# Fourteen priorities of a greedy scheduler that writes the order of every engine, in a hybrid decoder layer

## The chip, the cores and the metric

The kernel runs on one core of a Trainium2 chip. The metric is the device time of one execution in microseconds (us): the median of three runs of the kernel before is 645.49 us (645.2 to 647.72). The engines are TensorE (PE: matmuls and transposes), VectorE (DVE), ScalarE (ACT), GpSimd (POOL) and SyncE (SP, which only issues transfers). Each engine works through its own instructions strictly in the order in which the program lists them.

## The reference, cut to what matters

One layer on 512 tokens of width 1024, in float32:

- a norm and one input projection to 1816 columns: 512 for a state-space mixer (S5), 512 for the queries, 768 for keys and values of three attention branches, 24 for gates;
- the S5 mixer: a complex diagonal recurrence per 16-channel group, then GELU and a gated linear unit (GLU) with a 512 x 512 matrix;
- the attention: a compressed branch (31 block summaries), a selected branch and a window branch. At this length the selected and the window branch both come to full causal attention, each with its own keys and values. Each head's three results are mixed with sigmoid gates;
- two norms, the output projection, the residual;
- a mixture of experts: 4 groups, the best group per token, the best 2 of its 8 experts, each a gated MLP of inner width 256. The weights of all 32 experts are 100 MB and must all be read.

## The kernel before, in words

**How work is written.** Each part of the layer is a Python generator (`proj`, `scores`, `gelu`, ...). It yields one instruction at a time, or a `Seq` of matmuls, sometimes with several engines to choose from (`Any`, and `cp`, line 399 on, which offers ACT, DVE and sometimes POOL). It can also yield a condition (a buffer must be free, a flag must be set). All generators run interleaved in one planner, `Sched` (line 112). All instructions carry line 234 in the profile, the planner's `issue`.

**What sets the order.** The planner has a cost and a latency for every kind of instruction. For the next instruction of every generator that isn't held by a condition, `pick` finds the earliest time `s` at which its engine is free and its inputs are there. Then `run` takes the one with the least sum of start and priority, and writes it at the end of its engine's list (lines 299 and 300):

```
if best is None or s + h[1] < best[0]:
    best = (s + h[1], s, f, h)
```

`h[1]` is the generator's entry in `PRIO`. A lower number means: taken first. A priority of -0.6 against -0.1 wins where the other could start up to 0.5 us earlier, all in the planner's own time. A generator that waits for a flag is not in the comparison until the planner has written the instruction after which the flag is set.

**The stages.** (1) `wload`, `xsplit`, `wsplit` and `proj` make the projection in three-term float32r products; beside it run `s5` (tables of the recurrence), the sinks (`sink_u`, `sink_k`, `sink_q`, `sink_gt` for the gates) and `compress`. (2) S5 in four rounds r = 0 to 3: `s5a` (tables per round, four transposes each through PSUM kind `g`, evacuated as `EP<-g`), `s5in`, `s5b` (matmuls `g<-FT,w`, recurrence `w<-r,w` on DVE), `gelu` (steps `w<-w` of 128 x 512; after rounds 1 and 3 it transposes through `g` and copies out as `sa<-g`, 128 x 256), then `glu`, whose end opens ten more 1 MB slots (`sb`) beside the thirteen of `sa`. (3) Attention: `scores` (matmuls into `a`, row maximum, exponential into a tile P of 1 MB), `scale` (P times gate over row sum: `mx` steps on four columns, then four multiplies `sa<-sa,mx` of 128 x up to 512 per unit), `values` (transposes `t<-ident,sa`, evacuation `pts<-t`, matmuls `o<-pts,sa`), `cmp` (the compressed branch, tiles `ct`), `finish`. A unit is a query block (3 to 0), a branch and a head group; only four P tiles exist (`NP`), and `values` must read a unit before its P is free again. PSUM has three buffers of kind `a`, two of `t`, one of `o`, two of `g`, shared by all. (4) `wo` and `outproj` with `resid`; `norm2`, `top2` and `place` per block of 128 tokens, `route`, `weights`. (5) The experts: `static` for 16 tiles of 128 tokens (two experts each), `spill` for one overflow tile. Six tiles (`SC`) are added into the residual on PE by `scatter`; the others by an indirect transfer that adds into the output in memory.

**The weights of the experts.** `prefetch` (line 469) issues 96 transfers of 1 MB on SP's queue, each as soon as a slot is free beyond those that `need` keeps for other parts. `static` frees a slot when its matmuls have read it.

Of the kernel before, what the change touches and what calls it, by code (L numbers as in the profile page):

```python
# [27 lines left out]
for _n, _w in (("g1", 8), ("lre", 48), ("lim", 48), ("lst", 48), ("dsk", 8), ("bglu", 4), ("gq", 1),  # L28
# [16 lines left out]

PRIO = {"proj": -3.72, "wsplit": 0.29, "xsplit": -0.08, "norm1": 0.04, "sink_u": 0.55, "sink_q": -0.76,
        "sink_gt": 3.61, "sink_k": -0.06, "s5": 0.19, "s5a": -0.69, "bcload": -9.42, "toeplitz": -18.02,
        "s5in": -0.17, "gelu": -0.12, "s5b": -0.75, "glu": -1.41, "compress": -0.96, "scores": -0.93,  # L50
        "scale": 0.37, "values": -0.25, "cmp": 0, "finish": -0.24, "wo": -1.28, "outproj": 0.02, "resid": -0.73,
        "norm2": -29.18, "top2": -0.61, "weights": 1.96, "place": -109.89, "prep": 1.2, "route": -1.71,
        "consts": -11.11, "scatter": -0.86, "base": -5.49, "moe": 43.94, "master": -5.48, "start": -35.5,
        "wload": -4.37, "prefetch": 3.58, "static": 2.45, "spill": -2.7}

# [54 lines left out]
class Sched:  # L112
# [12 lines left out]
    def spawn(self, gen, bias=0.0):  # L125
        self.th.append([gen, PRIO.get(gen.__name__, 0.0) + bias, None, None])

# [1981 lines left out]
```

## Time and profile before

| what | value |
|---|---|
| median of three runs | 645.49 us |
| the profiled execution | 649.24 us, of it 647.4 us span |
| PE busy | 542.4 us (84%) |
| DVE busy | 369.0 us (57%) |
| ACT busy | 229.9 us (36%) |
| POOL busy | 126.5 us (20%) |
| read from memory / written | 138.9 MB / 13.6 MB |

The profiled execution lies 3.75 us above the median of the runs. The page cuts the span into 40 slices and gives each engine's busy share in tenths; a table of busy time by stage is made by giving the profile the stage limits. In a timeline row stand start, duration, engine, operation, output and inputs by the program's names with the shape, the number of instructions merged, and in brackets the engine's idle time before the row with what ended it.

### The profile page before, as it was taken

To read this page: it belongs to the slowest core of one execution; us is meant where nothing else is said; L and a number is where in the kernel's file an instruction comes from. 1 tells how busy PE (TensorE), PEld (TensorE's weight loads), DVE (VectorE), ACT (ScalarE), POOL (GpSimd) and SP (SyncE) were. 2 spreads that over 40 slices of the span, in tenths; PEclk is the share of its full clock that TensorE was granted. 3 is DMA by queue.
4 is the path that set the end of the run, shared out by engine and by line. 5 is a ranking of instruction groups with operands and counts; after the bars stand their busy time and mean duration, and the time that the engine had idled before them with its cause. 6 is when DMAs were issued, how large, how long until landed. Compare 5 with 4: busy or idle time off the path is not lost. (4 is left out here: it accounts for less than half of the span.)

```text
span 647.4 us, 8863 instructions
## 1 busy us (share of the span) xinstructions
PE 542.4 (84%) x3071; PEld 328.1 (51%) x3071; DVE 369.0 (57%) x1076; ACT 229.9 (36%) x513; POOL 126.5 (20%) x143
## 2 busy tenths in 40 slices
PE   3979968973968996999997369799999999999673
PEld 2869937862545665676686233344343443434120
DVE  6898989889897987978656951002141340414000
ACT  6425123453735764767233021124212122221001
POOL 1020110442620305003232021202101010211010
PEclk9979979995977997999999569989999999999887
DMA  6543444420201101614987958999999999999993
GB/s 202 156 134 102 112 123 114 135 62 8 42 5 36 42 26 58 266 66 139 411 344 265 376 195 313 382 391 386 420 388 397 409 387 420 387 420 352 326 316 53
DMA packets 39742, 148.40 MB, mean 229 GB/s; under 512 B 9488, under 2 KB 16528, under 8 KB 27024
## 3 DMA queue, kind: packets, MB, share of 16 engines
q1 hardware_dynamic: 32928, 129.46, 52.8%
q0 software_dynamic: 5040, 15.21, 9.5%
q10 hardware_dynamic: 1728, 3.15, 1.3%
q8 instruction: 25, 0.41, 0.3%
q14 instruction: 21, 0.17, 0.1%
HBM read 138.92 MB, written 13.60 MB: 236 GB/s over the span
## 5 line engine op out<-in xcount | busy, mean ns | idle before, releaser
L234 PE MATMUL a<-sa 128*128 128x256 f32 (+4 forms) x608 | 113.7, 330 | 18.9 <-ACT sa L234 14.5
L234 PEld LDWEIGHTS a<-sa 128*128 128x128 f32 (+1 forms) x608 | 86.8, 196 | 34.7 <-ACT sa L234 17.9
L234 PE MATMUL a<-sa,sb 128*64 128x512 f32 (+1 forms) x324 | 96.2, 594 | 1.3 <-DMA sa<-in_we 1.3
L234 DVE TENSOR_TENSOR h<-a,h 128x256 f32<-128x256 f32 x17 | 7.2, 425 | 132.2 <-ACT h L234 132.2
L234 PE MATMUL a<-sb 128*64 128x512 f32 (+1 forms) x204 | 73.5, 624 | 3.0 <-DMA sb<-in_we 3.0
L234 PE MATMUL a<-sa,hT 128*64 128x512 f32 (+1 forms) x168 | 57.0, 599 | 1.7 <-ACT hT L234 0.9
L234 PEld LDWEIGHTS a<-sa,sb 128*64 128x64 f32 (+1 forms) x324 | 29.5, 141 | 48.1 <-issue 45.4
L234 ACT ACTIVATE h<-a 128x256 f32<-128x256 f32 x17 | 6.5, 384 | 111.0 <-PE a L234 111.0
L234 POOL DMA_INDIRECT out<-sc,oi x10 | 16.0, 1600 | 124.9 <-ACT sc L234 80.2
L234 PEld LDWEIGHTS a<-sb 128*64 128x64 f32 (+1 forms) x204 | 22.0, 150 | 30.1 <-issue 24.8
L234 ACT ACTIVATE sb<-t 128x512 f32<-128x512 f32 x42 | 23.6, 595 | 23.2 <-PE t L234 22.8
L234 POOL DMA_INDIRECT sc<-h2d,gi x16 | 16.5, 1033 | 78.0 <-PE t L234 59.3
L234 PE MATMUL a<-sb,hT 128*64 128x512 f32 x80 | 30.1, 600 | 0.5 <-ACT hT L234 0.5
L234 ACT ACTIVATE sa<-a,mx 128x512 f32<-128x512 f32 (+3 forms) x48 | 27.1, 573 | 8.5 <-DVE mx L234 7.9
L234 PE MATMUL o<-sa 128*128 128x256 f32 x192 | 28.4, 284 | 1.1 <-DVE xr L234 1.1
L234 DVE SCALAR_TENSOR_TENSOR sa<-a,tabw,sa 128x512 fp32r<-128x512 f32 x12 | 9.0, 751 | 35.5 <-ACT sa L234 25.5
L234 DVE TENSOR_REDUCE mx<-a 128x1 f32<-128x512 f32 (+3 forms) x44 | 27.0, 635 | 3.0 <-PE a L234 3.0
L234 PE MATMUL g<-sb,sa 128*128 128x512 f32 x104 | 27.7, 404 | 0.0
L234 ACT ACTIVATE pts<-t 128x512 f32<-128x512 f32 (+1 forms) x35 | 20.4, 595 | 18.1 <-PE t L234 18.1
L234 PE MATMUL t<-ident,sc 128*128 128x128 f32 x136 | 21.7, 306 | 5.3 <-DMA sc<-h2d,g1i 4.1
L234 PEld LDWEIGHTS o<-sa 128*128 128x128 f32 x192 | 25.3, 191 | 1.6 <-DVE xr L234 1.5
L234 PEld LDWEIGHTS t<-ident,sc 128*128 128x128 f32 x136 | 16.6, 155 | 18.4 <-issue 13.0
(391 smaller groups left out, 1046.3 us busy)
## 6 DMA issues: line engine op xcount, KB each, us to landing
sa<-in_we SPq DMA_DIRECT2D x58, 1024.0 KB, 22.6
sb<-in_we SPq DMA_DIRECT2D x33, 1024.0 KB, 16.4
raw<-in_win SPq DMA_DIRECT2D x14, 512.0 KB, 3.8
sc<-in_we SPq DMA_DIRECT2D x5, 1024.0 KB
sb<-in_wout SPq DMA_DIRECT2D x6, 512.0 KB, 7.4
xr<-in_xt SPq DMA_DIRECT2D x4, 512.0 KB, 5.3
sa<-in_wck SPq DMA_DIRECT2D x8, 256.0 KB, 3.0
sa<-in_wcv SPq DMA_DIRECT2D x8, 256.0 KB, 3.6
```

The costliest lines, as they stand in the source:

```text
L234: inst = getattr(e.real, fn)(*a, **k)
```

## The change

Fourteen entries of `PRIO` get other numbers. Nothing else differs: the same instructions, tiles, buffers and transfers, in another order on each queue, and, where several engines were offered, perhaps on another engine.

```diff
-PRIO = {"proj": -3.72, "wsplit": 0.29, "xsplit": -0.08, "norm1": 0.04, "sink_u": 0.55, "sink_q": -0.76,
-        "sink_gt": 3.61, "sink_k": -0.06, "s5": 0.19, "s5a": -0.69, "bcload": -9.42, "toeplitz": -18.02,
-        "s5in": -0.17, "gelu": -0.12, "s5b": -0.75, "glu": -1.41, "compress": -0.96, "scores": -0.93,
-        "scale": 0.37, "values": -0.25, "cmp": 0, "finish": -0.24, "wo": -1.28, "outproj": 0.02, "resid": -0.73,
-        "norm2": -29.18, "top2": -0.61, "weights": 1.96, "place": -109.89, "prep": 1.2, "route": -1.71,
-        "consts": -11.11, "scatter": -0.86, "base": -5.49, "moe": 43.94, "master": -5.48, "start": -35.5,
-        "wload": -4.37, "prefetch": 3.58, "static": 2.45, "spill": -2.7}
+PRIO = {"proj": -19.73, "wsplit": 0.29, "xsplit": -0.08, "norm1": 0.04, "sink_u": 0.55, "sink_q": -0.76,
+        "sink_gt": 4.55, "sink_k": -0.06, "s5": 0.19, "s5a": -0.69, "bcload": -9.42, "toeplitz": -18.37,
+        "s5in": -0.41, "gelu": -0.13, "s5b": -0.75, "glu": -1.41, "compress": -0.96, "scores": -0.93,
+        "scale": -0.59, "values": -0.25, "cmp": -0.42, "finish": -0.24, "wo": -1.28, "outproj": 0.66,
+        "resid": -0.73, "norm2": -29.18, "top2": -0.61, "weights": 1.96, "place": -109.49, "prep": 1.2,
+        "route": -0.92, "consts": -11.18, "scatter": -4.3, "base": -5.49, "moe": 43.94, "master": -10.82,
+        "start": -35.5, "wload": -4.84, "prefetch": 3.58, "static": 2.45, "spill": -2.7}
```

The larger moves are `proj` (-3.72 to -19.73), `sink_gt` (3.61 to 4.55), `scale` (0.37 to -0.59), `cmp` (0 to -0.42), `outproj` (0.02 to 0.66), `route` (-1.71 to -0.92), `scatter` (-0.86 to -4.3) and `master` (-5.48 to -10.82). `toeplitz`, `s5in`, `gelu`, `place`, `consts` and `wload` move by at most 0.47.

## Rows read from the trace of the kernel before

**Rows 1.** The page: the span and its instructions, then busy us of each engine.
```profile
span 647.4 us, 8863 instructions
PE 542.4 (84%) x3071; PEld 328.1 (51%) x3071; DVE 369.0 (57%) x1076; ACT 229.9 (36%) x513; POOL 126.5 (20%) x143
```

**Rows 2.** Windows by stage: length, busy us (instructions) per engine, clock, DMA share, GB/s.
```profile
0.00:135.60 135.60, 110.32 (x830) 96.06 (x832) 118.37 (x328) 51.47 (x108) 25.48 (x48) 0.94 0.46 135
135.60:187.90 52.30, 32.47 (x261) 22.15 (x259) 47.84 (x122) 28.60 (x65) 19.92 (x23) 0.79 0.09 19
187.90:216.20 28.30, 23.98 (x183) 16.46 (x179) 23.49 (x67) 17.24 (x39) 4.51 (x3) 0.78 0.11 24
216.20:254.70 38.50, 31.74 (x169) 21.95 (x168) 31.39 (x63) 22.74 (x49) 13.45 (x11) 0.96 0.09 28
254.70:316.40 61.70, 60.72 (x328) 40.59 (x328) 49.63 (x152) 40.51 (x120) 8.75 (x14) 0.97 0.52 198
316.40:352.20 35.80, 34.51 (x187) 28.48 (x187) 23.93 (x107) 9.87 (x22) 10.22 (x8) 1.00 0.85 326
352.20:378.00 25.80, 6.72 (x58) 5.76 (x59) 19.79 (x126) 3.21 (x11) 4.77 (x4) 0.53 0.79 292
378.00:404.00 26.00, 24.77 (x114) 10.27 (x115) 6.84 (x33) 6.11 (x10) 4.84 (x5) 0.87 0.81 295
404.00:622.00 218.00, 205.96 (x921) 83.39 (x918) 47.29 (x81) 48.02 (x87) 31.42 (x26) 0.98 1.02 390
```

**Rows 3.** Timeline of SP, where the prefetch runs out of slots.
```profile
352.64 1.18 SPq L234 DMA_DIRECT2D sa<-in_we  x2
353.87 24.10 SPq L234 DMA_DIRECT2D sb<-in_we  x4
```

**Rows 4.** Timeline of DVE, 187.9 to 215 us.
```profile
188.44 3.54 DVE L234 TENSOR_SCALAR sa<-sa,mx 128x512 f32<-128x512 f32 x7
...
193.67 0.42 DVE L234 TENSOR_TENSOR ct<-g,mcmp 128x256 f32<-128x256 f32 x1
194.95 1.07 DVE L234 TENSOR_SCALAR sa<-g 128x256 f32<-128x256 f32 x2 [0.86 <-PE g L234]
...
198.43 0.48 DVE L234 TENSOR_SCALAR sa<-sa,mx 128x512 f32<-128x512 f32 x1
...
214.88 1.27 DVE L234 TENSOR_SCALAR sa<-sa,mx 128x512 f32<-128x512 f32 x3
```

**Rows 5.** Timeline of ACT: the last multiplies of the third unit.
```profile
199.90 1.32 ACT L234 ACTIVATE sa<-sa,mx 128x512 f32<-128x512 f32 x2
```

**Rows 6.** Timeline of PE, 190 to 202 us.
```profile
190.12 0.72 PE L234 MATMUL t<-ident,sa 128*128 128x128 f32 x4
191.93 0.66 PE L234 MATMUL g<-ident,yt 128*128 128x128 f32 x4 [1.09 <-ACT w L234]
...
196.17 1.08 PE L234 MATMUL g<-ident,EP 128*128 128x128 f32 x4 [1.26 <-DVE sa L234]
197.95 1.12 PE L234 MATMUL g<-ident,EP 128*128 128x128 f32 x4 [0.69 <-ACT EP L234]
...
201.65 2.58 PE L234 MATMUL t<-ident,sa 128*128 128x128 f32 x12
```

**Rows 7.** Windows within it: columns as in Rows 2.
```profile
190.00:193.90 3.90, 2.64 (x21) 1.93 (x18) 3.87 (x10) 3.34 (x8) 0.92 (x1) 0.94 0.04 8
193.90:200.70 6.80, 4.58 (x32) 3.29 (x34) 4.47 (x10) 3.32 (x7) 0.00 (x0) 0.50 0.33 70
```

**Rows 8.** Timeline of POOL: two multiplies of `scale`.
```profile
188.70 2.22 POOL L234 TENSOR_SCALAR sa<-sa,mx 128x512 f32<-128x512 f32 x1 [2.62 <-DVE mx L234]
...
213.52 1.56 POOL L234 TENSOR_SCALAR sa<-sa,mx 128x512 f32<-128x512 f32 x1 [10.21 <-DVE mx L234]
```

**Rows 9.** Timeline of PE: the end of `glu`, and `top2` before the last `outproj`.
```profile
252.98 1.86 PE L234 MATMUL g<-ones,sq 128*128 128x1 f32 x8 [5.43 <-POOL sq L234]
...
347.57 1.95 PE L234 MATMUL g<-sb 128*128 128x36 f32 x16
```

## The prediction

> **What bounds the kernel now.** I read the page first, then a table of busy time by stage, then the timelines of the engines in the stage where something waits. On the page [rows 1] no engine is busy all through: PE 84%, DVE 57%. The table by stage [rows 2] says why: the bound changes. From 404 to 622 us the transfers run without a gap (share 1.02, 390 GB/s) while DVE works 47 of 218 us; this is the reading of the expert weights, and no order of PE or DVE shortens it. From 352.2 to 378 us PE is busy for 6.7 of 25.8 us and DVE for 19.8: the routing, a chain of small DVE steps. Before that PE and DVE share the load: from 254.7 to 352.2 us PE stands at 95.2 of 97.5 us, so it is the bound there; from 135.6 to 254.7 us PE is busy for 88.2 of 119.1 us and DVE for 102.7, so PE often waits for DVE.
>
> The end of the front sets the end of the kernel. SP issued the last weight transfers for free slots just after 353.9 us, and the fourth of that row had to wait; the row lasts 24.1 us, to 378 [rows 3], when the first expert tile begins to free slots. The transfers were busy for 0.79 of 352.2 to 378 us and 0.81 of 378 to 404 us [rows 2], so 5.4 + 4.9 = 10.3 us of idle transfer time lie there, all of it behind the routing. If the routing ends x us earlier, the later stages move by x, up to about 10 us. So I count what the change does to the time at which the routing ends, and pass it on one to one.
>
> **The change part by part.**
>
> *proj, -16.0.* Among the generators that use PE while it runs, proj at -3.72 had the lowest number already (next compress, -0.96). It can now be put in front of PE work that could start up to 19 us sooner rather than 3. Its inputs come from wsplit, which is written in step with time, so it is rarely more than about a microsecond ahead. PE idles for 25.3 of the first 135.6 us [rows 2], the ceiling of any gain; a loss as large would need PE held for missing inputs again and again. I take 0, bounds -3 and +3: DVE, busy for 118.4 of these 135.6 us [rows 2], sets the pace of what proj reads, and PE's order is proj first either way.
>
> *scale, -0.96, with sink_gt, +0.94, and cmp, -0.42.* scale needs the gates, which sink_gt now delivers 0.94 later in the planner's order; scale then goes 0.96 sooner against everybody. The two cancel for its first instruction, so I leave 187.9 us where it is. After that scale stands ahead of gelu, cmp, values and finish, where it stood behind them; it stays behind s5a, s5b, scores and glu. What that does is visible: four units of query block 3 wait at 188 us. DVE does seven multiplies in 3.54 us [rows 4], POOL one in 2.22 us [rows 8]; then DVE turns to cmp (193.67), to the two copies of gelu's result (194.95, 1.07 us) and others, and gives one multiply at 198.43 [rows 4]; ACT ends the third unit at 199.90 + 1.32 = 201.2 us [rows 5]; the fourth is multiplied only from 213.5 us on [rows 4, 8]. The transposes of P stop on PE with the four at 190.12 us and resume at 201.65 us [rows 6]. At 3.54 / 7 = 0.51 us each, the four multiplies that are then left of the second and third unit put straight behind the seven end at about 192 + 4 x 0.51 = 194.0 us on DVE alone, some 7 us sooner.
>
> What PE can win from this is its idle time between: 3.90 - 2.64 + 6.80 - 4.58 = 3.5 us [rows 7]. I take -3.5; bounds 0 and -3.5 for the idle time alone. The granted clock is the second part: it was 0.50, the lower level of 1.2 GHz, from 193.9 to 200.7 us, after a stretch in which PE had idled. Work of 4.58 us done there would take 2.3 us at full clock. Whether the fall itself goes is open, since PE idles before 190 us too; I take half, -1.1, bounds 0 and -2.3. For the units of block 2, which also interleave with gelu, I take a further -0.5 (bounds 0 and -1.3, the 6.8 us of idle time from 216.2 to 254.7 less the 5.4 us of one wait [rows 2, 9]).
>
> The price is S5. The multiplies put ahead (four of the third unit, four of the fourth) are 8 x 0.51 = 4.1 us less what ACT and POOL take; gelu's copies at 194.95 free a PSUM buffer for which s5a's transposes at 196.17 waited [rows 6], and S5's last round and glu hang on those. So glu comes 0 to 4.1 us later. At its end PE waited 5.43 us already [rows 9]. As long as values and scores, now ahead, fill PE, this costs nothing; I take +1.0, bounds 0 and +4.1.
>
> In *Perfetto Trace Analysis*, section Optimizing Scalar/DVE Operations, the Trainium skill says that GpSimd and VectorE share a read port and that a DVE operation using two ports locks it, so that spreading work over both may not help. The trace leans that way: beside DVE's seven multiplies the one on POOL took 2.22 us, another 1.56 [rows 8]. Were two more multiplies to go to POOL at the longer time, by that rule the sum would lose 2 x 0.66 = 1.3 us of its gain and come to -2.8.
>
> *outproj, +0.64.* It stands further behind top2, values and finish. Before 352 us top2 has already been put in front of parts of outproj; one more piece, such as the 1.95 us at 347.57 [rows 9], may go ahead of the last block. That block's routing then starts later, but DVE, which bounds the routing, gets other blocks' steps sooner. I take 0, bounds -1 and +2.
>
> *scatter, -3.4.* It was ahead of static by 3.3 and is now by 6.8. PE work changes places inside 404 to 622 us, where transfers are the bound [rows 2]: 0; if a slot were freed late for it, +1.5; a gain I cap at -1.
>
> *master, -5.3; route, +0.8; toeplitz, s5in, gelu, place, consts, wload (at most 0.47).* master writes one fill on POOL, busy 10.2 of 35.8 us there [rows 2]; route still stands ahead of top2 and weights; the others change places with neighbours. 0 together, bounds -1 and +1.
>
> Sum: -3.5 - 1.1 - 0.5 + 1.0 = -4.1 us. For the profiled execution (647.4 us span, 649.24 in all) that is 645.1; it lies 3.75 us above the median, and against the median of 645.49 I forecast 641.4.
>
> **The rivals.**
>
> *S5 takes the gain back.* PE's idle time at 190 to 201 us is filled, but glu comes later by what scale took from DVE, and PE waits for it at 253 us instead. For it: DVE was busy for 23.5 of 28.3 us in this stage [rows 2], so one part's gain is another's wait. Against it: glu's first matmuls ran in the middle of scores and values, which could fill PE. Gain and price about cancel: -4 to -5 and +4.1; 645.
>
> *Slower, by the same mechanism at its upper end.* S5's delay of 4.1 us falls whole on the wait of 5.43 us at 253 us, the clock falls after it, and the idle time at 190 us stays, since the first waits there were for ACT and for S5's own transposes. A fall of the length seen from 193.9 to 200.7 us costs up to half of that, 3.4 us. 645.5 + 4.1 + half of 3.4 = 651.3. It decides once PE has no attention work left to put into glu's wait; 61.7 us of nearly full PE after 254.7 us [rows 2] speak against it.
>
> *A larger gain.* The new order also removes the wait of 5.43 us at 253 us: 645.5 - 3.5 - 2.3 - 5.4 = 634.3. For it: that wait sits on one in-order instruction behind POOL and needs only another neighbour. Against it: nothing in the change aims at POOL there.
>
> *The change does next to nothing*: the numbers of scale and sink_gt cancel everywhere, not just at the first instruction. Then 645.5; it counts with the first rival.
>
> **How the numbers follow.** Forecast 0.45, around 641.4, its own range 637.5 to 644.5. S5 takes it back, or nothing happens: 0.22, 643 to 648. Slower: 0.18, 649 to 655. Larger gain: 0.15, 631 to 637. About 0.5%, 3.2 us, is what a measurement can tell from no change, so faster means below 642.3 and slower above 648.7. Faster: 0.45 x 0.7 + 0.15 = 0.47. Slower: 0.18 and a little of the second case, 0.19. The same: 0.34. For 8 in 10 I cut the larger gain at 632.5 and the slower case at 651.3.
>
> **What would show it.** Right: in the profile after, DVE and ACT finish the third unit's multiplies before 197 us and the fourth's before 205; PE's transposes of P resume before 197 us; PE idles for less than 2 us from 190 to 201 us; the routing ends 3 to 5 us sooner and the stage of full transfers keeps its length. Wrong in the gain: PE's wait at the end of glu grows past 8 us, or the routing ends where it did. Wrong in the passing on: the routing ends sooner and the kernel doesn't, by transfer gaps after 404 us. Wrong at the root: the order before 187.9 us differs by more than a few instructions, or its length by more than 2 us.

## The result, and the profile after

The changed kernel takes 639.76 us (median of four runs, 637.21 to 640.31), the kernel before 646.61 us (four runs, 645.20 to 647.78): a ratio of 0.9887, 95% interval 0.985 to 0.9925. Forecast were 641.4 us and a range of 632.5 to 651.3. The total was met; most of the working behind it was not.

The profiled execution went from 649.24 us (span 647.4) to 639.9 us (span 638.1). Those 9.3 us are more than the 6.85 us between the medians, since the profiled execution of the kernel before lay 2.6 us above its median. The page after, in answer to [rows 1]: the span, then busy us of each engine.

```profile
span 638.1 us, 8840 instructions
PE 537.1 (84%) x3071; PEld 321.0 (50%) x3071; DVE 370.3 (58%) x1080; ACT 227.9 (36%) x509; POOL 124.3 (19%) x143
```

The table by stage after, in answer to [rows 2], cut near the same events (proj's end, the first step of `scale`, then values', outproj's and the routing's end); the engines stand in the order of the page.

```profile
0.00:136.70 136.70, 109.51 (x830) 95.20 (x832) 118.69 (x328) 51.22 (x107) 25.83 (x48) 0.95 0.46 134
136.70:191.40 54.70, 34.45 (x269) 23.35 (x267) 49.59 (x122) 28.31 (x64) 20.21 (x23) 0.81 0.08 18
191.40:216.20 24.80, 22.39 (x164) 14.37 (x160) 19.86 (x61) 18.59 (x42) 4.96 (x6) 0.80 0.12 27
216.20:254.70 38.50, 35.84 (x216) 22.98 (x213) 33.90 (x86) 29.32 (x68) 6.15 (x7) 1.00 0.09 29
254.70:305.70 51.00, 48.00 (x259) 30.10 (x257) 44.20 (x123) 33.83 (x99) 12.63 (x14) 1.00 0.55 210
305.70:351.30 45.60, 43.36 (x225) 35.20 (x224) 29.84 (x124) 8.15 (x23) 11.70 (x10) 1.00 0.78 317
351.30:374.00 22.70, 5.11 (x59) 4.36 (x60) 19.89 (x127) 2.21 (x8) 3.52 (x3) 0.58 0.76 284
...
400.00:613.00 213.00, 201.16 (x906) 82.06 (x906) 47.29 (x81) 47.30 (x86) 31.13 (x26) 0.98 1.02 389
```

Read by events, after minus before, the gain does not grow steadily: the first step of `scale` is 3.5 us later (187.9 to 191.4), values end 11.1 us earlier (316.4 to 305.3), outproj ends only 0.9 us earlier (351.4 to 350.5), the routing 4.2 us (378.2 to 374.0), the span 9.3 us. Values' 11.1 us are mostly not a gain: 8.9 us of PE work (43.4 - 34.5 us busy in the stage to outproj's end) now stand behind values instead of among them. About 5 us of that come from outproj's number, which fell behind theirs: with it put back (e6) the stage has 38.5 us of PE work. The routing stage is 3.1 us shorter than in [rows 2] (25.8 to 22.7), with the same DVE work in it (19.9 and 19.8 us). And 5.1 us come behind the routing. The prefetch issues its last transfer for a free slot at 353.5 us instead of 356.0, and the next one goes out at 373.4 instead of 377.6 us (SP's timeline after, to hold against [rows 3]):

```profile
353.47 0.83 SPq L234 DMA_DIRECT2D sb<-in_we  x1
373.44 0.34 SPq L234 DMA_DIRECT2D sc<-in_we  x1
```

At the place where I had put the gain, most of the signs that I had named are there. DVE's timeline after, against [rows 4]:

```profile
192.46 1.25 DVE L234 TENSOR_SCALAR sa<-sa,mx 128x512 f32<-128x512 f32 x3
...
193.86 2.04 DVE L234 TENSOR_SCALAR sa<-sa,mx 128x512 f32<-128x512 f32 x5
...
196.01 1.28 DVE L234 TENSOR_SCALAR sa<-sa,mx 128x512 f32<-128x512 f32 x3
197.20 0.42 DVE L234 TENSOR_TENSOR ct<-g,mcmp 128x256 f32<-128x256 f32 x1
```

ACT's timeline after, against [rows 5]:

```profile
193.88 1.95 ACT L234 ACTIVATE sa<-sa,mx 128x512 f32<-128x512 f32 x3 [0.67 <-DVE mx L234]
196.07 0.72 ACT L234 ACTIVATE sa<-sa,mx 128x512 f32<-128x512 f32 x1 [0.24 <-DVE mx L234]
```

Eleven multiplies on DVE come before `cmp` starts; the third unit is done at 195.9 us (201.2 before), the fourth at 197.3. PE's timeline after, against [rows 6] and [rows 9]:

```profile
195.26 1.30 PE L234 MATMUL t<-ident,sa 128*128 128x128 f32 x4 [1.02 <-ACT sa L234]
...
264.15 0.73 PE L234 MATMUL a<-sa 128*128 128x256 f32 x4 [1.17 <-ACT sa L234]
...
265.95 1.05 PE L234 MATMUL g<-ones,sq 128*128 128x1 f32 x8
```

The transposes of P resume at 195.3 us instead of 201.65, and the matmul of glu's norm, `g<-ones,sq`, which had stood behind 5.43 us of idle time, has none before it. The window of 190 to 201 us, before and then after:

```profile
190.00:201.00 11.00, 7.52 (x58) 5.52 (x56) 8.34 (x19) 6.96 (x14) 0.92 (x1) 0.66 0.22 47
```

```profile
190.00:201.00 11.00, 8.94 (x58) 5.82 (x56) 10.06 (x31) 7.19 (x14) 0.11 (x1) 0.50 0.01 1
```

PE idles for 2.1 us there instead of 3.5 (I had named less than 2). But the number of PE instructions is the same, 58, and the granted clock is lower, 0.50 instead of 0.66: the local profit is next to nothing.

### The profile page after: what moved, and what is told of

Read it like the earlier page. It is cut to its first block, busy times and chain, and to the rows that moved or that the text cites. A ratio compares the mean times of both kernels' runs of the same rounds, so it can differ in the third digit from the quotient of the medians.

```text
span 638.1 us, 8840 instructions
## 1 busy us (share of the span) xinstructions
PE 537.1 (84%) x3071; PEld 321.0 (50%) x3071; DVE 370.3 (58%) x1080; ACT 227.9 (36%) x509; POOL 124.3 (19%) x143
## 5 line engine op out<-in xcount | busy, mean ns | idle before, releaser
L234 PE MATMUL a<-sa,sb 128*64 128x512 f32 (+1 forms) x264 | 102.4, 603 | 4.0 <-DMA sa<-in_we 4.0
L234 PE MATMUL a<-sb 128*64 128x512 f32 (+1 forms) x232 | 98.0, 615 | 3.2 <-DMA sb<-in_we 3.1
L234 PE MATMUL a<-sa,hT 128*64 128x512 f32 (+1 forms) x176 | 63.7, 600 | 1.4 <-ACT hT L234 1.4
L234 PEld LDWEIGHTS a<-sb 128*64 128x64 f32 (+1 forms) x232 | 28.4, 144 | 37.7 <-issue 32.2
L234 POOL DMA_INDIRECT out<-sa,oi x10 | 16.0, 1600 | 123.0 <-ACT sa L234 80.2
L234 ACT ACTIVATE sa<-a,tabw 128x512 f32<-128x512 f32 (+1 forms) x32 | 22.0, 687 | 46.8 <-PE a L234 45.8
L234 PEld LDWEIGHTS a<-sa,hT 128*64 128x64 f32 (+1 forms) x176 | 17.7, 139 | 25.6 <-issue 22.8
L234 PE MATMUL g<-sb,sa 128*128 128x512 f32 x112 | 30.3, 405 | 0.0
L234 PE MATMUL t<-ident,sa 128*128 128x128 f32 (+1 forms) x160 | 26.4, 296 | 3.2 <-ACT pts L234 1.8
L234 ACT ACTIVATE sb<-t 128x512 f32<-128x512 f32 x39 | 22.0, 596 | 19.8 <-PE t L234 19.7
L234 PEld LDWEIGHTS t<-ident,sa 128*128 128x128 f32 (+1 forms) x160 | 18.2, 144 | 16.2 <-ACT pts L234 7.6
```

What stands on the lines that cost most here:

```text
L234: inst = getattr(e.real, fn)(*a, **k)
```

## The experiments

"Pair" means `scale` at -0.59 together with `cmp` at -0.42, and all else as before. Every kernel was timed beside the kernel before on the same chip, whose median was 647.47 (e1 to e4), 647.52 (e5 to e8) and 645.96 us (e9 to e12). The table has the ends of values (the last of their matmuls into `o`), of outproj and of the routing, and the span of the profiled execution, in us. "Tail" is the span less the routing's end. The last column tells when PE began the small matmul `t<-ones,oss` with which `finish` works out the last query block's norm.

| kernel | median | ratio (95%) | values | outproj | routing | span | tail | last `finish` |
|---|---|---|---|---|---|---|---|---|
| before | | | 316.4 | 351.4 | 378.2 | 647.4 | 269.2 | 320.8 |
| after | 639.76 | 0.9887 (0.985-0.9925) | 305.3 | 350.5 | 374.0 | 638.1 | 264.1 | 310.0 |
| e1, ten quiet | 647.05 | 0.9987 (0.997-1.0005) | 315.7 | 350.8 | 377.3 | 646.4 | 269.1 | 320.1 |
| e2, scale back | 661.26 | 1.0192 (1.0137-1.0246) | 328.0 | 366.4 | 391.4 | 664.4 | 273.0 | 335.6 |
| e3, gates back | 638.73 | 0.9845 (0.9802-0.9888) | 304.3 | 351.3 | 372.3 | 637.5 | 265.2 | 310.1 |
| e4, scale alone | 660.02 | 1.0207 (1.0164-1.0251) | 327.5 | 367.7 | 387.2 | 656.4 | 269.2 | 364.5 |
| e5, pair | 636.99 | 0.982 (0.9781-0.9859) | 308.3 | 345.7 | 369.4 | 635.2 | 265.8 | 314.2 |
| e6, outproj back | 638.09 | 0.985 (0.9828-0.9873) | 306.9 | 346.2 | 370.6 | 637.3 | 266.7 | 312.8 |
| e7, cmp back | 665.41 | 1.0292 (1.0266-1.0318) | 328.6 | 373.2 | 391.8 | 661.2 | 269.4 | 366.6 |
| e8, outproj alone | 667.36 | 1.0291 (1.0243-1.0338) | 330.7 | 375.4 | 394.1 | 665.8 | 271.7 | 369.1 |
| e9, cmp alone | 646.98 | 1.0014 (0.9986-1.0041) | 315.0 | 350.2 | 376.4 | 644.6 | 268.2 | 319.4 |
| e10, pair, block 3 | 649.25 | 1.006 (1.0025-1.0095) | 320.5 | 351.5 | 379.2 | 644.3 | 265.1 | 325.2 |
| e11, pair, other blocks | 655.49 | 1.0143 (1.0093-1.0194) | 323.7 | 361.9 | 386.6 | 654.4 | 267.8 | 328.4 |
| e12, fitted again | 627.28 | 0.9703 (0.9654-0.9753) | 300.0 | 336.0 | 359.8 | 627.3 | 267.5 | 304.4 |

**e1: the ten entries counted at nothing**, on the kernel before.

```diff
-"proj": -3.72, "toeplitz": -18.02, "s5in": -0.17, "gelu": -0.12, "place": -109.89,
-"route": -1.71, "consts": -11.11, "scatter": -0.86, "master": -5.48, "wload": -4.37,
+"proj": -19.73, "toeplitz": -18.37, "s5in": -0.41, "gelu": -0.13, "place": -109.49,
+"route": -0.92, "consts": -11.18, "scatter": -4.3, "master": -10.82, "wload": -4.84,
```

> The kernel before, with ten of the fourteen entries changed: proj, toeplitz, s5in, gelu, place, route, consts, scatter, master, wload. The order differs from before only in a handful of instructions near 50 us and near 140 us, and not at all from 165 us on. My prediction put all ten at 0 (bounds -5 to +7 in sum): ratio to before 1.000, within 0.3%. Rival, that proj in front of everybody or scatter in front of the experts is the gain: 0.989, like the full change.

0.9987: no difference that can be measured. What the change does has to be sought in the other four entries.

**e2 and e3: take `scale` out of the change, and the gates' number out of it.**

```diff
-        "scale": -0.59,
+        "scale": 0.37,
```

> The changed kernel with scale back at 0.37; thirteen entries stay new. If scale ahead of gelu and cmp is what wins (my prediction: -4.1 us with everything), the time goes back to that of before or above it, 646 to 650 us, and the third and fourth unit of query block 3 are again multiplied late, with PE waiting for them. Rival, that the gates and the order before 190 us win: it stays near 640 us.

```diff
-        "sink_gt": 4.55,
+        "sink_gt": 3.61,
```

> The changed kernel with sink_gt back at 3.61, so that the order up to the first scale is that of before (gates at about 180 us, queries at 163 us). If only scale, cmp and outproj matter the time stays at 640 us. If the new order before 190 us is the gain, it goes back to 646 us. If that order is a loss which the others outweigh, it falls below 640 us.

Without `scale` the change costs 1.9% (661 us where I had expected 646 to 650), so its three other entries together do harm. Without the gates' number it is as good as with it. That number had reordered much: on POOL the two steps of the gates now stand ahead of S5's table steps (`EP<-bc,AB`) and not behind them, and the gates are ready 15 us sooner, as POOL's timelines show, first before and then after.

```profile
179.71 0.77 POOL L234 TENSOR_TENSOR gatc<-gat,anyq 128x32 f32<-128x32 f32 x1
```

```profile
164.78 0.25 POOL L234 TENSOR_TENSOR gatc<-gat,anyq 128x32 f32<-128x32 f32 x1
```

All the same `scale` began 3.5 us later (191.4); in e3 it began at 187.5.

**e4: `scale` alone**, the mechanism on which the forecast rested.

```diff
-        "scale": 0.37,
+        "scale": -0.59,
```

> The kernel before with scale at -0.59 and nothing else. By my prediction's sum, -4 us without the offset of the gates: 641 to 643 us. Rival, that scale alone pushes cmp behind and needs cmp's number with it: no gain or a loss, 646 to 655 us, with the compressed branch late and values waiting for it.

A loss of 2.1%, to beyond the rival's range too. The mechanism of the forecast, alone, makes the kernel slower.

**e5, e7, e9: `cmp` with it, and `cmp` by itself.** e5 is the pair on the kernel before. e7 takes `cmp` out of the change, e9 is `cmp` alone.

```diff
-        "scale": 0.37, "values": -0.25, "cmp": 0,
+        "scale": -0.59, "values": -0.25, "cmp": -0.42,
```

> The kernel before with two entries changed: scale at -0.59 and cmp at -0.42. scale alone cost 2.1%, because cmp fell behind it. If the pair is the whole of the change: 638 to 641 us, ratio 0.985 to 0.992. If outproj's new number is needed too: above 643 us. If the pair still starves cmp: 650 us or more.

```diff
-        "cmp": -0.42,
+        "cmp": 0,
```

> The changed kernel with cmp back at 0, behind scale. If cmp is the partner that scale needs: 652 to 662 us, with the last step of cmp after 300 us and values waiting for it. If the order of cmp is hidden beside values: 640 us.

```diff
-        "cmp": 0,
+        "cmp": -0.42,
```

> The kernel before with cmp at -0.42 and nothing else, the fourth corner of the square whose others are: neither 647.5, scale alone 660, both 637 us. If the two act only together: 646 to 651 us. If cmp is what wins and scale only costs: 634 us or less.

The pair is the whole gain, 1.8%, with an interval that just overlaps that of the full change. `cmp` alone is worth nothing, and without `cmp` the change costs 2.9%. Four multiplies `sa<-ct,cmx`, one per query block, end `cmp`. The view of one tile gives their least, median and longest time in ns, and when the first started and the last ended: before, e4 (`scale` alone) and e5 (pair).

```profile
L234 DVE TENSOR_TENSOR sa<-ct,cmx x4: 424/424/426, 212.4 to 296.7; 128x256 f32<-128x256 f32 x4
```

```profile
L234 DVE TENSOR_TENSOR sa<-ct,cmx x4: 424/425/427, 229.3 to 323.8; 128x256 f32<-128x256 f32 x4
```

```profile
L234 DVE TENSOR_TENSOR sa<-ct,cmx x4: 424/424/424, 203.4 to 235.5; 128x256 f32<-128x256 f32 x4
```

With `scale` ahead and `cmp` left behind it, `cmp` loses DVE to it: its last step moves from 296.7 to 323.8 us, and values end 11.1 us later. `values` can't close a query block before it has the block's result of `cmp`: it transposes that and adds it into `o` on PE. Before, these transposes start 15 us or more after `cmp`'s last step of the block; in e4 they follow it by 0.3 to 1.7 us in all four blocks, in the last one so (PE's timeline in e4):

```profile
324.87 0.60 PE L234 MATMUL t<-ident,sa 128*64 128x128 f32 x4
```

Only then does `finish`, the mixing of the three branches, start for the block, and `finish` feeds outproj. With both entries moved, `cmp` is over by 235.9 us and values end 8.1 us earlier than before.

Where the pair's gain lies, PE's idle time tells. From 162 us to values' end it falls from 18.6 to 13.0 us, about as much as outproj ends earlier (5.7 us). At 190 to 201 us it falls by 1.6 us; the larger part, 5.3 us, lies between 240 and 270 us, where the wait of 5.43 us at glu's norm [rows 9] is gone. The windows before and with the pair:

```profile
240.00:270.00 30.00, 23.59 (x119) 17.66 (x119) 23.47 (x55) 17.50 (x42) 8.98 (x8) 0.89 0.46 175
```

```profile
240.00:270.00 30.00, 28.86 (x149) 18.71 (x147) 22.53 (x53) 18.71 (x48) 11.55 (x10) 1.00 0.17 63
```

The pair's span is 12.2 us shorter: 5.7 us at outproj's end, 3.1 in the routing stage, 3.4 behind it.

What a late `finish` then costs shows in DVE's timelines around the mixing of the last query block (`of,pkt` steps, then `oss<-of`), before and in e4:

```profile
317.45 1.14 DVE L234 SCALAR_TENSOR_TENSOR sb<-of,pkt,sa 128x128 fp32r<-128x128 f32 x4
...
320.26 0.29 DVE L234 TENSOR_TENSOR oss<-of 128x128 f32<-128x128 f32 x1
```

```profile
328.52 0.35 DVE L234 SCALAR_TENSOR_TENSOR sa<-of,pkt,sa 128x128 fp32r<-128x128 f32 x1
329.42 0.21 DVE L234 TENSOR_SCALAR sa<-sa 128x1 f32<-128x1 f32 x1 [0.55 <-ACT sa L234]
...
359.54 0.34 DVE L234 SCALAR_TENSOR_TENSOR sa<-of,pkt,sa 128x128 fp32r<-128x128 f32 x1
...
362.76 0.29 DVE L234 TENSOR_TENSOR oss<-of 128x128 f32<-128x128 f32 x1
```

In the kernel before, `finish` of the last block is through by 324.6 us, and `top2` (number -0.61 against -0.24) has its first DVE step only at 334.4. In e4 `finish` has done its first steps at 328.5 us when `top2` of the first block begins, at 329.4. From there `top2` of three blocks goes first: DVE does 124 steps, none of them of `finish`, which goes on at 359.5. The last block's outproj waits that long, and PE with it: e4's stage from values' end to outproj's end has 40.2 - 28.3 = 11.9 us of idle PE, that of before 0.5 us.

```profile
327.50:367.70 40.20, 28.27 (x153) 23.30 (x152) 32.06 (x149) 8.10 (x22) 10.70 (x9) 0.83 0.48 190
```

Some of it comes back, since the three blocks' routing steps are done by then: the routing stage is 19.5 us instead of 26.8.

**e6 and e8: outproj out of the change, and alone.**

```diff
-        "outproj": 0.66,
+        "outproj": 0.02,
```

> The changed kernel with outproj back at 0.02. My prediction had outproj at 0 (bounds -1 and +2): 638 to 640 us. Rival, that its later place is what shortened the routing stage from 25.8 to 22.7 us, because top2 of the other blocks got in front: 642 to 644 us. Other rival, that it delays the last block: 636 us or less.

```diff
-        "outproj": 0.02,
+        "outproj": 0.66,
```

> The kernel before with outproj at 0.66 and nothing else. By my prediction 0, bounds -1 and +2: 646 to 649 us. Rival, that outproj behind values starves the path to the last block or, through the buffers that it holds, the attention itself: 655 us or more.

Within the change outproj's number is worth nothing that shows (0.985 without, 0.9887 with it), though in the profiles outproj ends 4.3 and the routing 3.4 us later with it. Alone it costs 2.9%, the largest effect of any single entry tried, and the trace has the same picture as e4: values end at 330.7 us, after `top2` has begun (328.2), and between 343.0 and 366.2 us the last `finish` gets not one DVE step. The wait spreads to the transfers. The residual's stores (`out<-sb`) wait for outproj on the queue in which the prefetch stands behind them (three waits for DVE's `sb`, 35.5 us together): e8's SP timeline, then its window from just behind values' end to outproj's.

```profile
340.13 36.42 SPq L234 DMA_DIRECT2D out<-sb  x4
```

```profile
331.70:375.40 43.70, 29.45 (x134) 22.69 (x133) 32.36 (x142) 5.21 (x14) 9.06 (x7) 0.77 0.40 164
```

The DMA share is 0.40 where the kernel before had 0.85 [rows 2]. Why values end 14 us later in e8 is not settled.

**e10 and e11: the pair with `scale`'s new number in query block 3 only, and in the other blocks only.** e10 keeps exactly the multiplies that my sum had priced at -3.5 and -1.1 us.

```diff
-                self.spawn(self.scale(qb, br, g, pe[g], st[g]))
+                self.spawn(self.scale(qb, br, g, pe[g], st[g]), 0.0 if qb == 3 else 0.96)
```

> scale and cmp as in the pair, but scale at -0.59 only in the four units of query block 3 and at 0.37 in the others. My prediction put 4.6 of the gain's 5.1 us into block 3 (PE's idle time at 190 to 201 us and the clock): then 637 to 642 us. If the gain lies in the units of the blocks 2 and 1, which before waited until 242 and 298 us: 650 us or more, since cmp then stands ahead of those units.

```diff
-                self.spawn(self.scale(qb, br, g, pe[g], st[g]))
+                self.spawn(self.scale(qb, br, g, pe[g], st[g]), 0.96 if qb == 3 else 0.0)
```

> The opposite: scale at -0.59 in the units of the query blocks 2, 1 and 0, and at 0.37 in block 3, with cmp at -0.42. If the later blocks carry the gain: 636 to 640 us. If block 3 carries it, as I predicted: 646 us or more. If both are needed, because each late unit holds a P tile that the next scores need: 646 to 660 us here and in the other.

e10 does at 190 us all that I asked: the multiplies of the fourth unit are done by 194.0 us, PE idles for 2.4 us from 190 to 201 us, and the granted clock there is 1.00, the upper level of 2.4 GHz. DVE's timeline and the window of e10:

```profile
188.10 4.04 DVE L234 TENSOR_SCALAR sa<-sa,mx 128x512 f32<-128x512 f32 x10
...
192.75 1.28 DVE L234 TENSOR_SCALAR sa<-sa,mx 128x512 f32<-128x512 f32 x3
```

```profile
190.00:201.00 11.00, 8.63 (x84) 6.18 (x82) 10.38 (x28) 7.69 (x15) 0.00 (x0) 1.00 0.24 53
```

Yet it gains nothing (1.006). PE got 84 instructions done there instead of 58, and then waited for others: from 201 us to values' end it idles for 12.9 us where it had idled for 8.5 before, most of it between 240 and 270 us. The wait at glu's norm, which the pair removes, is still there (5.49 us). Its timeline in e10, at glu's end and after it, and the window:

```profile
257.79 1.87 PE L234 MATMUL g<-ones,sq 128*128 128x1 f32 x8 [5.49 <-POOL sq L234]
...
263.90 1.22 PE L234 MATMUL a<-sa 128*128 128x256 f32 x4 [2.94 <-ACT sb L234]
```

```profile
240.00:270.00 30.00, 21.47 (x96) 16.37 (x95) 22.13 (x60) 15.30 (x37) 10.73 (x9) 0.77 0.31 118
```

`cmp` alone (e9) left even less idle time at 190 to 201 us, 1.1 us, and gained nothing either. In e10 `cmp` also stands ahead of the later blocks' `scale`, so it isn't block 3 alone that it tests; by e9 that place of `cmp` costs nothing by itself.

e11 loses 1.4%; there PE waits in front of S5's transposes:

```profile
225.87 1.94 PE L234 MATMUL g<-ident,yt 128*128 128x128 f32 x8 [7.37 <-DVE yt L234]
```

So the gain needs `scale` ahead in all four blocks and `cmp` with it. From 162 us to values' end PE idles for 18.6 us before, 13.0 with the pair, 21.8 in e10, 23.2 in e11.

**e12: ten entries fitted again.** From the pair, ten entries around attention and routing were given new numbers.

```diff
-"sink_q": -0.76, "gelu": -0.12, "glu": -1.41, "scores": -0.93, "scale": -0.59, "cmp": -0.42,
-"finish": -0.24, "resid": -0.73, "norm2": -29.18, "top2": -0.61,
+"sink_q": -0.86, "gelu": -0.18, "glu": -1.61, "scores": -0.88, "scale": -0.38, "cmp": -0.33,
+"finish": -0.17, "resid": -0.55, "norm2": -28.61, "top2": -0.71,
```

> A version fitted from the pair: ten entries moved by 0.05 to 0.6 (scale -0.38, cmp -0.33, finish -0.17, resid -0.55, scores -0.88, sink_q -0.86, gelu -0.18, glu -1.61, top2 -0.71, norm2 -28.61). If the stages before the routing are shortened by closing PE's waits: 626 to 632 us, all of it before the experts, whose stage keeps its 250 to 260 us. If the pair's order was a lucky one: 637 us or more.

0.9703: better than both kernels, and than the pair. PE idles for only 10.0 us from 162 us to values' end, and not at all from 240 us on. Which of the ten entries does it, no run tells. Windows of e12 from 162 us to values' end, then to outproj's, the routing's and the span's end:

```profile
162.00:300.00 138.00, 128.04 (x795) 84.99 (x795) 118.92 (x320) 101.53 (x257) 37.68 (x42) 0.96 0.28 96
300.00:336.00 36.00, 35.03 (x180) 28.38 (x180) 26.27 (x116) 7.72 (x20) 9.04 (x8) 1.00 0.83 337
336.00:359.80 23.80, 7.47 (x80) 6.55 (x78) 21.09 (x121) 2.78 (x11) 6.08 (x6) 0.59 0.94 361
359.80:627.30 267.50, 239.33 (x1066) 96.28 (x1066) 54.23 (x114) 56.33 (x101) 39.32 (x33) 0.96 0.96 359
```

## Why the total was right and the working was not

**What bounds the kernel: right, and the strongest part.** In all fourteen kernels the tail is 264 to 273 us long, while the routing's end moves over 34 us (359.8 to 394.1). Whoever ends the routing earlier has the gain: in each of them 19 or 20 of the 96 transfers of weights are issued 2 us before the routing's end, and the others wait for slots. The ceiling of "about 10 us" was wrong: e12's routing ends 18.4 us earlier and its span is 20.1 us shorter. I had taken the idle transfer time for the limit, but in e12 the transfers come earlier too (share 0.94 in the routing stage, 0.79 before). One reading was off: the transfer that went out at 377.6 us had waited 17.4 us for a DVE step of the routing, not for the first expert tile, whose first matmul with weights began at 383.0 us.

**The ten quiet entries at 0: right** (e1). `scatter` and `master` are in it.

**`scale` and `sink_gt` cancel, and the order before 187.9 us stays: wrong**, by the mark that I had set. The gates came 15 us earlier, not 0.94 later, and the first `scale` was 3.5 us later. I had subtracted two numbers; what a number does is decided by whom it lets pass, and here the gates came to stand ahead of S5's steps on POOL. By which way a higher number led to that isn't shown. By e3 it is worth nothing in the end.

**-3.5 and -1.1 at 190 to 201 us: this is the step that failed.** It had the right place of entry and the wrong account. The signs on the multiplies and the transposes were met (third unit before 197, fourth before 205, transposes before 197), and only 1.4 of the 3.5 us of idle time went. The clock fell all the same, to 0.50 over the whole window. e10 shows that the account fails even where the clock is mended and the idle time shrinks by 1.1 us: PE idles for 4.4 us more behind it. What the pair gains before the routing lies mostly in the wait of 5.43 us at glu's norm, which my sum had left as it was and only the rival of a larger gain had priced. I had priced one block's gap as if PE's later work were the bound from there on; with DVE busy for 102.7 of 119.1 us [rows 2], PE was to wait somewhere. The -0.5 for the other blocks was too small: without them there is no gain (e10). POOL, which I had feared to slow, took no multiply of `scale` from 186 to 218 us after; so the rule of the Trainium skill that I had weighed (*Perfetto Trace Analysis*, section Optimizing Scalar/DVE Operations) was not put to the test, and no run here shows its price.

**`cmp` at no cost beside `scale`: wrong, and it is the main omission.** My sentence put `scale` ahead of "gelu, cmp, values and finish" and asked only what S5 would lose. The one that lost was `cmp`: moved along, -1.8%; left behind, +2.1% (e4, e7). My slower rival, 651.3, had the right sign for `scale` alone but the wrong mechanism: not glu, but `cmp`, and behind it `finish` under `top2`.

**The price of S5 at 0 to 4.1 us, and where it would show.** glu ended 13.2 us later (257.2 to 270.4), three times my bound. It cost nothing that shows, as I had said it might: attention filled PE, and the wait of 5.43 us went too. So the rival "a larger gain" was right about the wait, not about the sum.

**outproj at 0, bounds -1 and +2: wrong by far alone** (+2.9%, e8), near enough within the change (e6). I had asked what one piece of outproj would cost, not whom the later outproj lets pass. That `finish` stands 0.37 behind `top2` had been in the table of numbers from the start. Before, it does no harm since `finish` is through 10 us before `top2` begins. In e4, e7 and e8 values end 11 to 14 us later than before, and the last `finish` reaches PE 44 to 48 us later. This reading rests on their traces; no run moved `finish` ahead of `top2` in one of them, so it isn't shown by an edit. e2 and e10 are caught in part (their last `finish` has a gap of 32 and 26 us on DVE, after its matmul on PE). e11 isn't caught, and is slow for another reason.

**The routing stage: counted at 0, measured at -3.1 us**, and the same in the pair (by the table of ends 26.8 before, 23.5 after, 23.7 in e5). The traces tell where it went. In the kernel before, ACT's square of the last block's tokens, which `top2` needs, waits 7.19 us for a store of normed tokens, and DVE's first step of that block's `top2` waits 3.23 us for the square (ACT's and DVE's timelines):

```profile
354.37 0.63 ACT L234 ACTIVATE sc<-sb 128x512 f32<-128x512 f32 x1 [7.19 <-DMA h2d<-sc]
356.21 0.21 DVE L234 TENSOR_SCALAR sb<-sb 128x1 f32<-128x1 f32 x1 [3.23 <-ACT sc L234]
```

After, in the pair and in e12 DVE has no such wait: it idles for 2.7 to 2.8 us of the stage instead of 6.0, with 20.7 to 21.1 us of work instead of 20.8. In e1 and e9, with stages about as long as before, the wait is there (2.9 and 2.6 us). e10 lacks it and is long all the same, 27.7 us, because DVE has 23.1 us of work left there. No edit moves the store alone, so this is read and not tested.

**Passed on one to one: nearly.** 4.2 us at the routing became 9.3 in the profiles. PE's timelines at the overflow tile, before and after, show the shift at the wait for its gather, and at its last transposes of `h`.

```profile
419.24 1.97 PE L234 MATMUL t<-ident,sc 128*128 128x128 f32 x8 [4.11 <-DMA sc<-h2d,g1i]
...
435.84 0.38 PE L234 MATMUL g<-ident,h 128*128 128x128 f32 x2
```

```profile
413.11 1.95 PE L234 MATMUL t<-ident,sc 128*128 128x128 f32 x8 [3.61 <-DMA sc<-h2d,g1i]
...
428.26 0.38 PE L234 MATMUL g<-ident,h 128*128 128x128 f32 x2
```

The shift is 6.1 us at the first and 7.6 at the second. From there it stays: the last step of `scatter` ends at 582.9 instead of 590.5, 7.6 us earlier. The last 1.7 us come behind that. e1, whose order differs little from that of before, has the same tail (269.1), and the medians differ by 6.85 and not 9.3 us; how much of these 5 us is the order's and how much the single execution's, the runs don't tell.

In short, the forecast was right by luck, by two errors that met: a gain that isn't where I put it, and a partner of it that I had not counted.

## What to carry to other kernels

Priorities in a greedy order don't add up: here +2.1% and nothing make -1.8% together, and one entry's +2.9% vanishes beside the others. So before pricing a step that is moved ahead on a busy in-order engine, list who stands between its old and its new number, and follow each of them to the one that waits for it; test the pairs, not only the single edits. And idle time filled in one place is a gain only if PE doesn't wait for as long at a later one, so take the gain at the last join (here the routing's end), and name in advance the place where the time would come back.

## What was unexpected

A late part costs nothing up to a point and much behind it. Where values ended by 316.4 us, `finish` was through before `top2` began, and nothing was lost by it; in e4, e7 and e8, with values' end 11 to 14 us later, the kernel was 2 to 3% slower.

In the window of 190 to 201 us 58 PE instructions, not all the same ones, were busy for 8.94 us at a granted clock of 0.50 after and for 7.52 us at 0.66 before; e10 did 84 in 8.63 us at 1.00. The fall of the clock that I wanted to avoid was deeper in the faster kernel.
